# Turning attention heads for a two-layer trunk: per token tile in split form, or two heads at a time as plain float32 rows

## The chip, the cores and the metric

The kernel runs on one core of one Trainium2 chip. The metric is the device time of one execution in microseconds (us), as the median of several runs. TensorE (PE) multiplies matrices, VectorE (DVE), ScalarE (ACT) and GpSimd (POOL) do the elementwise work, and SyncE (SP) issues most of the DMAs. PE writes into PSUM banks of 128 partitions x 512 float32 values; ACT and DVE empty them into SBUF.

## The reference, cut to what matters

Two layers, each a half feed-forward, a mixer and another half feed-forward, on 512 tokens of width 1024 in float32. The mixer projects the normalised input once and feeds three kinds of attention. The change concerns the query and key heads between projection and scores:

```python
proj = h @ w_in
(qa, ka, va, qi, ki, wi, qb, kb, vb, qc, kc, vc, ga, gb, gc) = jnp.split(proj, offsets, axis=-1)
qa = rope(rmsnorm(qa.reshape(B, S, A_HEADS, HEAD_DIM), qk_g[0]), cos, sin)
...
sc = jnp.einsum('bqhcd,bshcd->bhcqs', qb, k) * scale
```

Projection leaves tokens on the partitions and heads along the free dimension. Scores need the head dimension (64) on the partitions and tokens along the free dimension, so every query and key head has to be transposed.

## The kernel before

**Precision.** Matrix products run in the one-pass type float32r. To keep float32 accuracy each operand is carried as two parts, `hi` (the value rounded to float32r) and `lo` (the rest), and a product is the sum of three matmuls (`mm3`, L227 to L229; in the projections L758 to L760).

**Heads.** A turned head is a 128x512 tile `dst[h]`: hi of the 64 head values on one half of the partitions, lo on the other half, tokens along the row. `scores` (L843) multiplies a query tile with the key tile and with a copy whose halves are exchanged by two DMAs (`swapped`, L837), which gives all four products of hi and lo.

**Groups.** Per layer there are five groups of heads: `qi` (8 index queries, token tiles 1 to 3), `ki` (1 index key), `b` (8 heads), `c0` and `c1` (8 each), `a` (5). A group is projected by `project` (L745): for each token tile of 128, 24 matmuls into an `mm` bank, handed out in four pieces of six. Then ACT copies the result out with the norm's scale, the norm of the heads (`normed`, L777) and the rotation (`rope`, L765, on POOL) follow.

**Turning, to_heads (L817).** For each token tile, `lag` turns of the main loop after its projection (4 for `qi` and `ki`, 7 for the others), `split` writes hi with ACT (L822) and lo with DVE (L823) into a tile `st`, [head][hi, lo][64]. Three turns later (`LAG_H`) `turn` transposes each head (L829): one 128x128 float32r transpose per head and token tile, four heads to a PSUM bank `tr`, two banks for eight heads. Each head's 128x128 block is then copied to `dst[h]` by whichever of ACT and DVE is assigned (`nc.any`, L832).

**The main loop** (end of `mixer`) does in each turn: `tick()`, which issues the deferred steps that are due; one unit of attention work if there is credit (index scores, then attention b, c0, c1, a, each when its heads are `ready`); picks of the top-k choice at 0.36 a turn, all on DVE (L1004, L1005); then one piece of dense work, the first in the list `dense` whose condition holds. Everything issued by the first three is held behind the last dense matmul (`behind`), and a planner puts each engine's instructions in a fixed order at build time. Attention transposes its probabilities with plain float32 128x128 transposes (`turned`, L863, transposes at L870, copies at L872), in the same three `tr` banks.

**Buffers.** PSUM has 2 banks `mm`, 3 `sc`, 3 `tr`. `st` has two buffers, the rows `v` of the heads share the tag `t1` (three buffers).

Of the kernel before, what the change touches and what calls it, by code (L numbers as in the profile page):

```python
# [36 lines left out]
T1 = 3  # L37
P0 = 4
P1 = 2
PT = 6  # L40
ST = 2
RAW = 4
QL = 4
HL = 4
# [3 lines left out]
RATE = 1  # L48
PICKS = 0.36
LAG_I, LAG_N = 4, 7  # L50
LAG_S, LAG_H = 4, 3
LAG_T, LAG_C, LAG_V = 3, 5, 2
AHEAD = 4
FF_PARTS = [4, 4, 4, 4, 6]
# [25 lines left out]
def trunk_kernel(ctx, tc, xt_in, pos_in, ng_in, wgu, wdn, wgrp, wgate, wbr_s, wbr_c, wo, qkg_in, lam_in, subg_in, out):  # L80
# [34 lines left out]

    ident = const.tile([P, P], F32, name="ident")
    make_identity(nc, ident)
    ident_r = const.tile([P, P], F32R, name="ident_r")
    V.tensor_copy(ident_r, ident)
# [114 lines left out]
    class Norm:  # L234
# [80 lines left out]
        def diagonals(self):  # L315
            parts = sm.tile([P, 2, NT, 1], F32R, name=nm("rnp"), tag="rnp", bufs=1)
            V.tensor_copy(parts[:, 0], self.rn)
            V.tensor_tensor(parts[:, 1], self.rn, parts[:, 0].bitcast(F32), op=ALU.subtract)
            self.dg = [tmp.tile([P, T], F32R, tag=tag, name=nm("dg"), bufs=b) for tag, b in (("t1", T1), ("t2", 2))]
            for e, dg in enumerate(self.dg):  # L320
                V.tensor_tensor(dg.rearrange("p (t q) -> p t q", t=NT), ident_r[:, None, :].bitcast(F32).to_broadcast([P, NT, P]),
                                parts[:, e].bitcast(F32).to_broadcast([P, NT, P]), op=ALU.mult)

        def broadcast(self):
# [407 lines left out]
    def mixer(l, n, nxt, aside):  # L732
# [44 lines left out]
        def normed(o, t, spec):  # L777

            nh = sum(s[1] for s in spec)
            v = temp("t1", bufs=T1).rearrange("p (h d) -> p h d", d=HD)  # L780
            S.activation(v[:, :nh], o[:, :nh * HD].rearrange("p (h d) -> p h d", d=HD), AF.Copy, scale=n.rn[:, t, :])
            sq = temp("t0")
            S.activation(sq[:, :nh * HD].rearrange("p (h d) -> p h d", d=HD), v[:, :nh], AF.Square)
            ss = sm.tile([P, 8, 1], F32, name=nm("ss"), tag="ss")
            V.reduce_sum(ss[:, :nh, 0], sq[:, :nh * HD].rearrange("p (h d) -> p h d", d=HD), axis=AX.X)
            V.tensor_scalar(ss[:, :nh, 0], ss[:, :nh, 0], 1.0 / HD, EPS, op0=ALU.mult, op1=ALU.add)
            G.tensor_tensor(ss[:, :nh, 0], ss[:, :nh, 0], neghalf[:, :nh], op=ALU.pow)

            def scaled():
                V.tensor_tensor(v[:, :nh], v[:, :nh], ss[:, :nh].to_broadcast([P, nh, HD]), op=ALU.mult)  # L790
                h0 = 0
                for row, hn in spec:
# [21 lines left out]
                for _, fn in due:  # L814
                    fn()

        def to_heads(v, nh, t, dst, lag, done):  # L817

            s = phase[-1].tile([P, 8, 2, HD], F32R, tag="st", name=nm("st"), bufs=ST)

            def split():
                S.activation(s[:, :nh, 0, :], v[:, :nh], AF.Copy)  # L822
                V.tensor_tensor(s[:, :nh, 1, :], v[:, :nh], s[:, :nh, 0, :].bitcast(F32), op=ALU.subtract)  # L823
                defer(LAG_H, turn)

            def turn():
                ps_ = [bank("tr") for _ in range(0, nh, 4)]
                for h in range(nh):
                    PE.transpose(ps_[h // 4][:, h % 4 * P:(h % 4 + 1) * P].bitcast(F32R),  # L829
                                 s[:, h].rearrange("p a d -> p (a d)"), ident_r)  # L830
                for h in sorted(range(nh), key=lambda h: (h % 4, h)):
                    nc.any.tensor_copy(dst[h][:, t * P:(t + 1) * P], ps_[h // 4][:, h % 4 * P:(h % 4 + 1) * P])  # L832
                done[0] += 1

            defer(lag, split)

        def swapped(src):  # L837
            d = slot(F32R)
# [80 lines left out]
        va = phase[-1].tile([P, NT, HD], F32, tag="va", name=nm("va"), bufs=1)  # L919

        def dense_qi():
            for t, o in project("qi", range(1, NT)):
# [4 lines left out]
                v = temp("t1", bufs=T1).rearrange("p (h d) -> p h d", d=HD)  # L927
# [5 lines left out]
        def dense_ki():  # L933
            for t, o in project("ki"):
                if o is None:
                    yield True
                    continue
                v = temp("t1", bufs=T1).rearrange("p (h d) -> p h d", d=HD)
                S.activation(v[:, 0], o[:, :HD], AF.Copy, scale=n.rn[:, t, :])
                rope(v[:, :1], t, 1)  # L940
                to_heads(v, 1, t, kis, LAG_I, ready["i"])
# [4 lines left out]
        ready = {k: [0] for k in ("i", "b", "c0", "c1", "a")}  # L946

        def dense_qk(name, rows, qs, ks):
            for t, o in project(name):
                if o is None:  # L950
                    yield True
                    continue
                v = normed(o, t, [(base + rows[0], 4), (base + rows[1], 4)])
                to_heads(v, 8, t, qs + ks, LAG_N, ready[name])
                yield True

        def dense_vc():
            for t, o in project("vc"):
# [3 lines left out]
                S.activation(vc(t), o, AF.Copy, scale=n.rn[:, t, :])  # L962
                yield True

        def dense_a():
            for t, o in project("a"):
                if o is None:
                    yield True
                    continue
                v = normed(o, t, [(base + 0, 4), (base + 1, 1)])  # L970
                to_heads(v, 5, t, qa + ka, LAG_N, ready["a"])
                S.activation(va[:, t, :], o[:, 320:384], AF.Copy, scale=n.rn[:, t, :])
                yield True

# [172 lines left out]
        def finished(b):  # L1147

            if b not in outs:
# [10 lines left out]
        work = deque([  # L1160
            (lambda: ready["i"][0] == 2 * NT - 1, index_scores()),
            (lambda: ready["b"][0] == NT,
             attend("b", qb, kb, None, causal_mask, lambda j, h: vb(j)[:, h * HD:(h + 1) * HD], on_b)),
            (lambda: ready["c0"][0] == NT, attend_c(qc0, kc0, 0, on_c[:2])),
            (lambda: ready["c1"][0] == NT, attend_c(qc1, kc1, 1, on_c[2:])),
            (lambda: ready["a"][0] == NT and len(masks) == NT,
             attend("a", qa, ka * 4, ka2, lambda i: masks[i], lambda j, h: va[:, j, :], on_a)),
        ])

# [121 lines left out]
```

## Time and profile before

| | |
|---|---|
| median of 3 runs | 2293.15 us (2291.82 to 2294.11) |
| the profiled execution's own time | 2294.2 us |
| its span | 2292.4 us |
| granted TensorE clock over the span | 0.999 of full speed |
| first mixer stage, roughly | 366 to 756 us |
| second mixer stage, roughly | 1502 to 1892 us |

The span is the time from the first to the last recorded instruction. A busy share is the time in which an engine had an instruction under way. Matmuls overlap their neighbours, so a PE that is busy all the time is not by that at its peak; what one block of matmuls costs is read from the starts of the matmuls around it. The two mixer stages run the same program, so one is read and the result doubled.

### The profile page before, as it was taken

To read this page: it belongs to the slowest core of one execution; us is meant where nothing else is said; L and a number is where in the kernel's file an instruction comes from. 1 tells how busy PE (TensorE), PEld (TensorE's weight loads), DVE (VectorE), ACT (ScalarE), POOL (GpSimd) and SP (SyncE) were. 2 spreads that over 40 slices of the span, in tenths; PEclk is the share of its full clock that TensorE was granted. 3 is DMA by queue.
4 is the path that set the end of the run, shared out by engine and by line. 5 is a ranking of instruction groups with operands and counts; after the bars stand their busy time and mean duration, and the time that the engine had idled before them with its cause. 6 is when DMAs were issued, how large, how long until landed. Compare 5 with 4: busy or idle time off the path is not lost.

```text
span 2292.4 us, 35928 instructions
## 1 busy us (share of the span) xinstructions
PE 2266.5 (99%) x13605; PEld 2002.1 (87%) x13605; DVE 1717.4 (75%) x3104; ACT 1110.6 (48%) x2097; POOL 384.7 (17%) x501
## 2 busy tenths in 40 slices
PE   9999999999999999999999999999999999999999
PEld 7899988888888889999889999888888887899997
DVE  7777765798965777777687777658999657777774
ACT  5544435666534454444444444456764344444442
POOL 0111101364011111110011101033631110110100
PEclk9999999999999999999999999999999999999999
DMA  4656525322232455655256555243322224655552
GB/s 169 181 155 162 141 66 168 96 78 84 79 97 82 135 152 154 163 156 141 77 151 166 160 145 158 76 135 83 93 76 91 88 83 138 166 157 149 150 139 65
DMA packets 111646, 286.74 MB, mean 125 GB/s; under 512 B 13168, under 2 KB 13168, under 8 KB 111472
## 3 DMA queue, kind: packets, MB, share of 16 engines
q1 hardware_dynamic: 89584, 245.21, 33.8%
q0 software_dynamic: 20736, 37.76, 9.8%
q8 instruction: 107, 1.75, 0.3%
q10 hardware_dynamic: 1152, 1.47, 0.2%
q14 instruction: 67, 0.55, 0.1%
HBM read 270.76 MB, written 6.29 MB: 121 GB/s over the span
## 4 chain that ended last, share of the span: by engine, by line
PE 86%; DVE 7%; DMA 2%; ACT 2%; issue 1%; POOL 1%; SPq 0%; ACTq 0%; DVEq 0%; POOLq 0%
PE mm L227 11%; PE mm L229 11%; PE mm L228 11%; PE sc L227 8%; PE sc L229 8%; PE sc L228 8%; PE tr L227 5%; PE tr L229 5%; PE tr L228 5%; PE mm L758 3%; PE mm L759 3%; PE mm L760 3%; PE sc L847 1%; PE sc L848 1%; DVE lo L344 1%
## 5 line engine op out<-in xcount | busy, mean ns | idle before, releaser
L227 PE MATMUL mm<-h,hi 128*128 128x512 f32 x1216 | 481.0, 396 | 1.5 <-DVE h L547 0.8
L229 PE MATMUL mm<-h,lo 128*128 128x512 f32 x1216 | 475.3, 391 | 4.3 <-DVE lo L344 4.3
L228 PE MATMUL mm<-h,hi 128*128 128x512 f32 x1216 | 474.4, 390 | 0.0
L452 POOL DMA_DIRECT2D sa<-in_wgu x144 | 126.5, 1050 | 929.9 <-DMA sa<-in_wgu 449.9
L229 PEld LDWEIGHTS mm<-h,lo 128*128 128x128 f32 x1216 | 228.3, 188 | 54.8 <-DVE lo L344 6.1
L344 DVE TENSOR_TENSOR lo<-raw,hi 128x1024 fp32r<-128x1024 f32 (+1 forms) x198 | 232.9, 1179 | 56.1 <-ACT hi L341 55.7
L227 PEld LDWEIGHTS mm<-h,hi 128*128 128x128 f32 x1216 | 228.4, 188 | 47.8 <-issue 3.4
L227 PE MATMUL sc<-h,hi 128*128 128x256 f32 (+1 forms) x832 | 264.9, 318 | 0.0
L228 PEld LDWEIGHTS mm<-h,hi 128*128 128x128 f32 x1216 | 228.6, 188 | 41.2
L229 PE MATMUL sc<-h,lo 128*128 128x256 f32 (+1 forms) x832 | 263.6, 317 | 0.0
L228 PE MATMUL sc<-h,hi 128*128 128x256 f32 (+1 forms) x832 | 263.3, 316 | 0.0
L341 ACT ACTIVATE hi<-raw 128x1024 fp32r<-128x1024 f32 (+1 forms) x198 | 200.5, 1020 | 88.2 <-PE tr L228 56.2
L227 PE MATMUL tr<-h,hi 128*128 128x256 f32 (+1 forms) x704 | 214.3, 304 | 3.7 <-ACT hi L572 1.8
L229 PE MATMUL tr<-h,lo 128*128 128x256 f32 (+1 forms) x704 | 213.6, 303 | 0.0
L228 PE MATMUL tr<-h,hi 128*128 128x256 f32 (+1 forms) x704 | 213.3, 303 | 0.0
L220 ACT ACTIVATE hi<-raw 128x1024 fp32r<-128x1024 f32 (+2 forms) x136 | 139.6, 1029 | 96.1 <-PE mm L228 58.4
L221 DVE TENSOR_TENSOR lo<-raw,hi 128x1024 fp32r<-128x1024 f32 (+2 forms) x136 | 172.7, 1271 | 16.7 <-ACT hi L220 15.9
L227 PEld LDWEIGHTS sc<-h,hi 128*128 128x128 f32 x832 | 158.8, 191 | 12.8 <-ACT hi L572 0.5
L228 PEld LDWEIGHTS sc<-h,hi 128*128 128x128 f32 x832 | 158.9, 191 | 11.9
L229 PEld LDWEIGHTS sc<-h,lo 128*128 128x128 f32 x832 | 158.7, 191 | 10.8 <-DVE lo L573 0.2
L227 PE MATMUL sc<-h,qhi 128*128 128x256 f32 x576 | 162.6, 282 | 4.2 <-ACT e L485 2.2
L758 PE MATMUL mm<-hi,h 128*128 128x512 f32 (+2 forms) x432 | 165.3, 383 | 0.0
(331 smaller groups left out, 5027.8 us busy)
## 6 DMA issues: line engine op xcount, KB each, us to landing
raw<-in_wgu SPq DMA_DIRECT2D x102, 512.0 KB, 4.6
sa<-in_wgu SPq DMA_DIRECT2D x72, 512.0 KB, 3.9
sa<-in_wgu POOLq DMA_DIRECT2D x144, 256.0 KB, 5.9
raw<-in_wdn SPq DMA_DIRECT2D x128, 256.0 KB, 4.0
raw<-in_wgate SPq DMA_DIRECT2D x48, 512.0 KB, 3.6
raw<-in_wgrp SPq DMA_DIRECT2D x40, 512.0 KB, 4.7
a<-in_wgu SPq DMA_DIRECT2D x72, 256.0 KB, 5.0
raw<-in_wdn SPq DMA_DIRECT2D x32, 384.0 KB, 3.7
```

What stands on the lines that cost most here:

```text
L220: S.activation(hi[:, sl], raw[:, sl], AF.Copy)
L221: V.tensor_tensor(lo[:, sl], raw[:, sl], hi[:, sl].bitcast(F32), op=ALU.subtract)
L227: PE.matmul(o, ah, bl, start=first, stop=False, skip_group_check=onto)
L228: PE.matmul(o, ah, bh, start=False, stop=False, skip_group_check=onto)
L229: last_mm[0] = PE.matmul(o, al, bh, start=False, stop=last, skip_group_check=onto)
L341: S.activation(self.h, self.src, AF.Copy)
L344: V.tensor_tensor(self.l, self.src, self.h.bitcast(F32), op=ALU.subtract)
L452: G.dma_start(self.sa[:, j * 512:(j + 1) * 512], src[:, 1536:], accum_op=ALU.add)
L758: PE.matmul(o[:, :w_cols], xl, wh[:, sl], start=k == 0, stop=False)
L759: PE.matmul(o[:, :w_cols], xh, wh[:, sl], start=False, stop=False)
L760: last_dense[0] = PE.matmul(o[:, :w_cols], xh, wl[:, sl], start=False, stop=k == KD - 1)
L847: PE.matmul(o, ql, k2[:, :(i + 1) * P], start=True, stop=False)
```

## The change

The heads are kept as plain float32 rows until all token tiles of a group are there (new tag `hv`, six buffers; for `ki` a slot of the large pool). Then, `lag` turns of the loop after the last tile, one pair of heads is turned in each turn of the loop: for each of the four token tiles (three for `qi`) one float32 transpose of 128 tokens x two heads of 64, all into one `tr` bank, which then holds head h on partitions 0 to 63 and head h+1 on 64 to 127, with all 512 tokens along the row. hi and lo are made while the bank is emptied: ACT copies each half to its place in `dst` (rounded to float32r), DVE subtracts that from the bank and writes lo to the other half of the partitions. Heads at odd places so have hi and lo exchanged, queries and keys alike.

`split`, `st`, `LAG_H` and `ident_r` go. The readiness conditions count heads in place of token tiles. Group `c1` may start only when group `a` has not begun or has all its tiles.

```diff
-        def to_heads(v, nh, t, dst, lag, done):
-            s = phase[-1].tile([P, 8, 2, HD], F32R, tag="st", name=nm("st"), bufs=ST)
-            def split():
-                S.activation(s[:, :nh, 0, :], v[:, :nh], AF.Copy)
-                V.tensor_tensor(s[:, :nh, 1, :], v[:, :nh], s[:, :nh, 0, :].bitcast(F32), op=ALU.subtract)
-                defer(LAG_H, turn)
-            def turn():
-                ps_ = [bank("tr") for _ in range(0, nh, 4)]
-                for h in range(nh):
-                    PE.transpose(ps_[h // 4][:, h % 4 * P:(h % 4 + 1) * P].bitcast(F32R),
-                                 s[:, h].rearrange("p a d -> p (a d)"), ident_r)
-                for h in sorted(range(nh), key=lambda h: (h % 4, h)):
-                    nc.any.tensor_copy(dst[h][:, t * P:(t + 1) * P], ps_[h // 4][:, h % 4 * P:(h % 4 + 1) * P])
-                done[0] += 1
-            defer(lag, split)
+        def head_rows():
+            return phase[-1].tile([P, 8, HD], F32, tag="hv", name=nm("hv"), bufs=HV)
+
+        def to_heads(vs, nh, dst, lag, done):
+            t0, t1 = min(vs) * P, (max(vs) + 1) * P
+            def turn(h):
+                both = h + 1 < nh
+                o = bank("tr")
+                for t, v in vs.items():
+                    PE.transpose(o[:HD * (1 + both), t * P:(t + 1) * P], v[:, h:h + 1 + both].rearrange("p a d -> p (a d)"), ident)
+                rows = slice(0, HD), slice(HD, P)
+                for e in range(1 + both):
+                    S.activation(dst[h + e][rows[e], t0:t1], o[rows[e], t0:t1], AF.Copy)
+                for e in range(1 + both):
+                    V.tensor_tensor(dst[h + e][rows[1 - e], t0:t1], o[rows[e], t0:t1], dst[h + e][rows[e], t0:t1].bitcast(F32),
+                                    op=ALU.subtract)
+                done[0] += 1 + both
+            for h in range(0, nh, 2):
+                defer(lag + h // 2, lambda h=h: turn(h))
...
-                to_heads(v, 8, t, qis, LAG_I, ready["i"])
+                if t == NT - 1:
+                    to_heads(vs, 8, qis, LAG_I, ready["i"])
...
-                 (lambda: units["b"] == 16, dense_qk("c1", (4, 5), qc1, kc1)), (lambda: 1 in outs, gated(1)),
+                 (lambda: units["b"] == 16 and len(rows_a) in (0, NT), dense_qk("c1", (4, 5), qc1, kc1)), (lambda: 1 in outs, gated(1)),
...
-            (lambda: ready["i"][0] == 2 * NT - 1, index_scores()),
-            (lambda: ready["b"][0] == NT,
+            (lambda: ready["i"][0] == 9, index_scores()),
+            (lambda: ready["b"][0] == 8,
```

## Rows read from the trace of the kernel before

**Rows 1.** The page, part 1: busy time, share of the span and instructions by engine.

```profile
PE 2266.5 (99%) x13605; PEld 2002.1 (87%) x13605; DVE 1717.4 (75%) x3104; ACT 1110.6 (48%) x2097; POOL 384.7 (17%) x501
```

**Rows 2.** Busy time by stretch: stretch, its length, each engine's busy us (instructions).

```profile
500.00:566.00 66.00, 63.91 (x368) 53.30 (x366) 59.99 (x168) 44.47 (x132) 37.29 (x53) 1.00 0.33 101
566.00:640.00 74.00, 72.94 (x373) 60.19 (x372) 67.98 (x185) 36.06 (x85) 8.86 (x12) 1.00 0.27 82
```

**Rows 3.** Timeline of PE, an eight-head float32r block: start us, length us, engine, line, tiles.

```profile
375.60 0.79 PE L829 MATMUL tr<-ident_r,st 128*128 128x128 f32 x8
376.23 0.47 PE L758 MATMUL mm<-hi,h 128*128 128x512 f32 x1
376.54 0.39 PE L759 MATMUL mm<-hi,h 128*128 128x512 f32 x1
```

**Rows 4.** Timeline of PE, a block of four plain float32 transposes (probabilities).

```profile
461.54 0.60 PE L870 MATMUL tr<-ident,p 128*128 128x128 f32 x4
461.89 0.48 PE L758 MATMUL mm<-hi,h 128*128 128x512 f32 x1
462.21 0.40 PE L759 MATMUL mm<-hi,h 128*128 128x512 f32 x1
462.44 0.40 PE L760 MATMUL mm<-lo,h 128*128 128x512 f32 x1
```

**Rows 5.** Groups by line and form, 366 to 756 us: count | busy us, mean ns.

```profile
L829 PE MATMUL tr<-ident_r,st 128*128 128x128 f32 x144 | 15.4, 244 | 0.0
L870 PE MATMUL tr<-ident,p 128*128 128x128 f32 x120 | 18.8, 273 | 0.9 <-DVE p L1056 0.9
L872 ACT COPY pt<-tr 128x512 f32<-128x512 f32 x9 | 5.1, 579 | 1.5 <-PE tr L870 1.4
L872 ACT COPY pt<-tr 128x384 f32<-128x384 f32 x8 | 3.7, 472 | 0.9 <-PE tr L870 0.8
L872 DVE COPY pt<-tr 128x384 f32<-128x384 f32 x4 | 2.2, 550 | 0.4 <-PE tr L870 0.4
L872 DVE COPY pt<-tr 128x512 f32<-128x512 f32 x3 | 2.1, 686 | 1.0 <-PE tr L870 0.9
```

**Rows 6.** Busy time by stretch of line L823 alone (the lo part, DVE).

```profile
500.00:566.00 66.00, 4.19 (x7) 1.00 0.33 101
...
sum 390.00, DVE 13.13; mean DVE 2.19
```

**Rows 7.** The same of line L832 (the copies out of the bank): DVE, then ACT.

```profile
500.00:566.00 66.00, 1.11 (x4) 10.41 (x48) 1.00 0.33 101
...
sum 390.00, DVE 8.95 ACT 25.04; mean DVE 1.49 ACT 4.17
```

**Rows 8.** The same of line L822 (the hi part, ACT), 366 to 640 us.

```profile
sum 274.00, ACT 12.52; mean ACT 1.57
```

**Rows 9.** Timeline of PE, where it stood still: [idle us before, what ended it].

```profile
510.76 1.53 PE L897 MATMUL tr<-pt,h 128*64 128x128 f32 x24 [1.21 <-ACT pt L872]
...
547.74 0.30 PE L870 MATMUL tr<-ident,p 128*128 128x128 f32 x1 [0.87 <-DVE p L1056]
...
566.92 0.94 PE L882 MATMUL tr<-h,pt 128*128 128x128 f32 x6 [0.62 <-ACT pt L872]
```

**Rows 10.** The chain that ended last, 500 to 566 us: start us, us, what.

```profile
510.23 0.48 ACT pt L872
...
535.38 0.88 ACT h L832 x6
```

**Rows 11.** Timeline of ACT, the split of the last tile of group a.

```profile
509.76 0.47 ACT L822 ACTIVATE st<-t 128x320 fp32r<-128x320 f32 x1 [1.51 <-POOL t L775]
```

**Rows 12.** Timeline of DVE, three instructions in the stretch of group c1.

```profile
546.65 0.68 DVE L823 TENSOR_TENSOR st<-t,st 128x512 fp32r<-128x512 f32 x1
547.25 0.34 DVE L1056 SCALAR_TENSOR_TENSOR p<-p,f,p 128x128 f32<-128x128 f32 x1
...
550.40 0.76 DVE L1068 TENSOR_SCALAR h<-h,css 128x128 f32<-128x128 f32 x1 [1.02 <-POOL css L1067]
```

**Rows 13.** Timeline of PE, the transposes of the last two tiles of group ki.

```profile
397.86 0.22 PE L829 MATMUL tr<-ident_r,st 128*128 128x128 f32 x1
...
403.45 0.22 PE L829 MATMUL tr<-ident_r,st 128*128 128x128 f32 x1
```

More of the change, by code (lines that the diff above doesn't have):

```diff
@@ L40 @@
 PT = 6
-ST = 2
+HV = 6
 RAW = 4
@@ L50 @@
 LAG_I, LAG_N = 4, 7
-LAG_S, LAG_H = 4, 3
+LAG_S = 4
 LAG_T, LAG_C, LAG_V = 3, 5, 2
@@ L117, in trunk_kernel @@
     make_identity(nc, ident)
-    ident_r = const.tile([P, P], F32R, name="ident_r")
-    V.tensor_copy(ident_r, ident)
     one = const.tile([P, 1], F32, name="one")
@@ L921, in dense_qi @@
         def dense_qi():
+            vs = {}
             for t, o in project("qi", range(1, NT)):
@@ L926, in dense_qi @@
                 n.advance(last_dense[0])
-                v = temp("t1", bufs=T1).rearrange("p (h d) -> p h d", d=HD)
+                v = vs[t] = head_rows()
                 S.activation(v, o.rearrange("p (h d) -> p h d", d=HD), AF.Copy, scale=n.rn[:, t, :])
                 rope(v, t, 8)
-                to_heads(v, 8, t, qis, LAG_I, ready["i"])
+                if t == NT - 1:
+                    to_heads(vs, 8, qis, LAG_I, ready["i"])
                 yield True
         def dense_ki():
+            vs = {}
+            kv = slot()[:, :NT * HD].rearrange("p (t d) -> p t d", d=HD)
             for t, o in project("ki"):
@@ L937, in dense_ki @@
                     continue
-                v = temp("t1", bufs=T1).rearrange("p (h d) -> p h d", d=HD)
+                v = vs[t] = kv[:, t:t + 1]
                 S.activation(v[:, 0], o[:, :HD], AF.Copy, scale=n.rn[:, t, :])
-                rope(v[:, :1], t, 1)
-                to_heads(v, 1, t, kis, LAG_I, ready["i"])
+                rope(v, t, 1)
+                if t == NT - 1:
+                    to_heads(vs, 1, kis, LAG_I, ready["i"])
                 S.activation(vb(t), o[:, 64:320], AF.Copy, scale=n.rn[:, t, :])
@@ L948, in dense_qk @@
         def dense_qk(name, rows, qs, ks):
+            vs = {}
             for t, o in project(name):
@@ L952, in dense_qk @@
                     continue
-                v = normed(o, t, [(base + rows[0], 4), (base + rows[1], 4)])
-                to_heads(v, 8, t, qs + ks, LAG_N, ready[name])
+                vs[t] = normed(o, t, [(base + rows[0], 4), (base + rows[1], 4)])
+                if t == NT - 1:
+                    to_heads(vs, 8, qs + ks, LAG_N, ready[name])
                 yield True
@@ L963, in dense_vc @@
                 yield True
+        rows_a = {}
         def dense_a():
+            vs = rows_a
             for t, o in project("a"):
@@ L969, in dense_a @@
                     continue
-                v = normed(o, t, [(base + 0, 4), (base + 1, 1)])
-                to_heads(v, 5, t, qa + ka, LAG_N, ready["a"])
+                vs[t] = normed(o, t, [(base + 0, 4), (base + 1, 1)])
+                if t == NT - 1:
+                    to_heads(vs, 5, qa + ka, LAG_N, ready["a"])
                 S.activation(va[:, t, :], o[:, 320:384], AF.Copy, scale=n.rn[:, t, :])
@@ L1160, in mixer @@
         work = deque([
-            (lambda: ready["i"][0] == 2 * NT - 1, index_scores()),
-            (lambda: ready["b"][0] == NT,
+            (lambda: ready["i"][0] == 9, index_scores()),
+            (lambda: ready["b"][0] == 8,
              attend("b", qb, kb, None, causal_mask, lambda j, h: vb(j)[:, h * HD:(h + 1) * HD], on_b)),
-            (lambda: ready["c0"][0] == NT, attend_c(qc0, kc0, 0, on_c[:2])),
-            (lambda: ready["c1"][0] == NT, attend_c(qc1, kc1, 1, on_c[2:])),
-            (lambda: ready["a"][0] == NT and len(masks) == NT,
+            (lambda: ready["c0"][0] == 8, attend_c(qc0, kc0, 0, on_c[:2])),
+            (lambda: ready["c1"][0] == 8, attend_c(qc1, kc1, 1, on_c[2:])),
+            (lambda: ready["a"][0] == 5 and len(masks) == NT,
              attend("a", qa, ka * 4, ka2, lambda i: masks[i], lambda j, h: va[:, j, :], on_a)),
```

4 lines of the change are left out of this document (2 added, 2 removed).

## The prediction, made before the result was known

> **What bounds the kernel now.** I read the page's busy times first: PE is busy 99% of the span, DVE 75%, ACT 48% [rows 1]. A busy PE can still be a slow one, so I went to PE's timeline in the first mixer stage and took distances between starts: matmuls of the projections start 0.23 us after one another without holes (462.21 to 462.44, [rows 4]), and the places where PE stood still are few, the largest 1.21, 0.87 and 0.62 us [rows 9]. So PE sets the time nearly everywhere, and work taken from it is worth its own length, as long as the others keep up. That is in doubt in one stretch: from 500 to 640 us DVE is busy 59.99 of 66 us and 67.98 of 74 us [rows 2]; PE's three halts lie there, released by ACT and DVE [rows 9], and the chain that ended last leaves PE and runs over ACT and DVE, over the head copies among others [rows 10]. Both layers have the same two stages, so I work out one mixer and double it.
>
> **PE: the transposes.** A block of eight float32r transposes starts at 375.60, the next matmul at 376.23 and the one behind it at 376.54 [rows 3]. The normal distance is 0.23, so the block costs 0.94 - 0.23 = 0.71 us: 0.63 us, or 0.079 for each transpose, and 0.08 once for the change over. Per layer there are 144 of them [rows 5]: 15 blocks of eight (three tiles of qi, four each of b, c0, c1), four blocks of five (a) and four single ones (ki), 23 blocks. 144 x 0.079 + 23 x 0.08 = 13.2 us.
>
> The new transposes are plain float32, 128 tokens by two heads of 64, which is the form in which the probabilities are turned already, 120 times per layer [rows 5]. Four of these start at 461.54, the matmul after next at 462.21 [rows 4]: 0.67 - 0.23 = 0.44 us for a block of four, change over included. After the change there are four blocks of three (qi; about 0.33 us) and 16 of four (ki 1, b, c0, c1 4 each, a 3): 4 x 0.33 + 16 x 0.44 = 8.4 us. **PE saves 4.8 us per layer, 9.6 us in all.** The two kinds of single-head block (ki, the fifth head of a) have only 64 columns; I price them as full ones, and their error is below 0.2 us a block.
>
> A page speaks against this. The Trainium skill, "FP8 and Floating Point Precision", section TensorE Precision Notes, has true float32 take four passes through the array. Were that so for these transposes, each would cost 4 x 0.079 = 0.32 us, the 76 new ones with 20 change overs 25.6 us per layer, and the kernel would be 25 us slower (an estimate with the page's factor). The row on the same form does not agree: 0.44 us for four.
>
> **ACT: relieved.** It loses the hi part (12.52 us per layer, [rows 8]) and its share of the copies (25.04 us, [rows 7]), 37.6 us. It gets one copy of 64x512 per head (64x384 for qi). The trace has none with 64 partitions; the nearest rows are the copies from the same kind of bank with 128, 0.579 us for 512 columns and 0.472 for 384 [rows 5]; the half of the partitions could cost anything from half of that to the same, and I take the same, because the length of the row is what differs between those two rows. 30 x 0.579 + 8 x 0.472 = 21.1 us: 16 us less per layer. Off the path it is worth nothing by itself; on the chain it stands at a few places only.
>
> **DVE: burdened, and in bursts.** It loses the lo part (13.13 us, [rows 6]) and 8.95 us of copies [rows 7], 22.1 us. It gets 38 subtractions out of PSUM. No row shows one that writes to other partitions than it reads; the nearest rows are 0.686 us for 512 columns out of a bank and 0.550 for 384 [rows 5]. 30 x 0.686 + 8 x 0.550 = 25.0 us, 2.9 us more per layer (between 10 us less, if half the partitions took half the time, and somewhat more). What matters is where: in 500 to 566 us it now has 4.19 + 1.11 = 5.3 us of head work [rows 6, 7]; after, c1 (8) and a (5) put 13 x 0.686 = 8.9 us there, 3.6 us more in a stretch that has 6 us of idle DVE. And the eight of a group no longer come spread over four tiles (16 turns of the loop) but in four turns in a row.
>
> How DVE overlaps its instructions weighs here. The lo part at 546.65 is 0.68 long and the next starts 0.60 later [rows 12], so 0.08 is hidden. The Trainium skill, "VectorE: DVE Perf Modes", section Two Vector instructions with no wait between them, has an instruction start only when all earlier ones have finished if its first partition differs from that of the last one's input or output. The new subtractions jump between the halves, so by it each pair would lose about three overlaps. No run here shows that yet. Three times 0.08 is 0.24 us for a pair, 1.4 us for the six pairs in that stretch; I leave it out of the sum and let it weigh in the rival below.
>
> **Order.** The index scores need the last turn of ki, which came 4 + 3 turns of the loop after its projection and now comes after 4. Two successive transposes of ki lie four turns apart, 397.86 and 403.45 [rows 13], 1.4 us a turn; so the index scores, the picks and all attention start three turns, some 4.2 us, earlier against the dense work. That is no gain to PE, whose total is the same, but it gives DVE a start for the tight stretch. The groups with lag 7 are ready when they were (7 + 3 turns then, the fourth pair at 7 + 3 now). The new condition on c1 costs at most a turn or two: attention b ends by my count within a turn of a's last tile. The six row buffers suffice by the same count: a's third tile needs a row of c0, whose last pair is turned two turns earlier.
>
> **A wait moved.** ACT's split of a's last tile waited 1.51 us for POOL's rotation [rows 11], and the copy behind it in ACT's queue let PE stand 1.21 us [rows 9, 10]. Now the first pair's transposes come at that same lag, and it is PE itself that would wait for POOL, with the projections queued behind it; in turn ACT's queue is free. Between 1.5 us lost and 1.2 us won per layer; I take nothing.
>
> **The sum.** 2294.2 - 9.6 = 2284.6 if all keep up. Against that I set 1.75 us per layer, about half of DVE's 3.6 us, for halts in the tight stretch: its idle time and its earlier start cover part, but much of its idle time is waiting in order on POOL (1.02 us at 550.40, [rows 12]) and can't all be filled. 2294.2 - 9.6 + 3.5 = 2288.1 for the profiled execution, whose time lies 1.05 us above the median; **2287.0 us** against the median, 6 us or 0.27% less.
>
> **The rivals.**
> DVE takes it all back. If the bursts push DVE past PE in c0, a and c1, the added 3.6 us and the 1.4 us of lost overlap land on the path, and the saving after 500 us (c1 and part of a, some 1.5 us) is hidden: 4.8 - 1.5 - 5.0 = -1.7 us per layer at the worst, 2296.5; at the mild end 2288.6. For it speaks the share of DVE, against it its earlier start and ACT's relief. Chance 0.30, no measurable change.
>
> The three tr banks are held too long, and it is slower. A new bank is held for two copies and two subtractions, 2 x 0.579 + 2 x 0.686 = 2.5 us, against some 1.4 us a turn. In four turns (5.6 us, 16.8 us of three banks) a burst needs 4 x 2.5 = 10 and attention's own transposes and products about 3: it fits. It decides at about 1 us of lateness of DVE (4 x 3.5 + 3 = 17); at 2 us late, four banks need 18 + 3 = 21, and PE waits (21 - 16.8) = 4.2 us in place, with all projections behind it. In two of the three bursts that fall into attention (c0, a, c1): 8.4 - 4.8 = 3.6 us per layer, 2300 us; in all three 2308. For it speaks that a burst asks 5.5 us of DVE in four turns on top of a share of 80%; against it, that fewer banks are taken than before (one per pair in place of two per tile). Chance 0.19; the four passes above have 0.01 of it besides, 0.20 for slower.
>
> The relief is worth more than the burden: the halts that ACT caused go (1.21 and 0.62, [rows 9]), and DVE's start covers its burst. 9.6 + 2 x 1.8 = 13.2, 2280 us. Chance 0.10.
>
> **How the numbers follow.** Forecast (2283 to 2288.5) 0.40, relief 0.10, taken back 0.30, slower 0.20. What a measurement of this kernel can tell from no change is about 0.2%, 4.6 us: faster 0.50, same 0.30, slower 0.20. The range leaves out the lower half of the relief case and the upper half of the slower one: 2281 to 2301. The likeliest case alone is 2283 to 2288.5.
>
> **What would show it.** PE: blocks of four at about 0.44 us and 152 of them. DVE: subtractions near 0.69 us and a busy sum some 6 us higher in all; ACT's sum some 33 us lower. First index score some 4 us earlier after ki's last tile. If the halts of PE between 480 and 570 us add up to more than 5 us per layer, with DVE or the tr banks as what ended them, the forecast is wrong. So it is if a transpose of two heads costs clearly more than 0.11 us.

## The result, and the profile after

The changed kernel takes 2336.93 us (2334.16 to 2337.72), before beside it 2294.11 us (2291.82 to 2296.76): a ratio of 1.0185, 95% interval 1.0174 to 1.0197. It is 43 us **slower**; I had forecast 2287.0 and a range up to 2301. The profiled execution has a time of its own of 2334.16 us and a span of 2332.4, at a mean granted clock of 0.994 (before: 2294.2, 2292.4, 0.999).

First the terms that I had priced. The page's part 1 of the changed kernel answers [rows 1]:

```profile
PE 2277.6 (98%) x13469; PEld 2005.4 (86%) x13469; DVE 1725.0 (74%) x3075; ACT 1089.4 (47%) x1897; POOL 384.6 (16%) x501
```

PE has 136 transposes fewer, DVE 7.6 us more, ACT 21.2 us less. PE's time without work over the span grows from 25.9 to 54.8 us. The groups by line and form, whole span (count | busy us, mean ns of one | idle time in front of them), answer [rows 5]:

```profile
L833 DVE TENSOR_TENSOR h<-tr,h 64x512 fp32r<-64x512 f32 x60 | 41.3, 688 | 11.7 <-ACT h L831 10.6
L831 ACT ACTIVATE h<-tr 64x512 fp32r<-64x512 f32 x60 | 35.5, 592 | 22.7 <-PE tr L828 22.2
L828 PE MATMUL tr<-ident,hv 128*128 128x128 f32 x136 | 24.0, 292 | 18.1 <-DVE ss L784 10.5 <-POOL hv L773 7.6
L833 DVE TENSOR_TENSOR h<-tr,h 64x384 fp32r<-64x384 f32 x16 | 8.9, 555 | 6.3 <-ACT h L831 6.1
```

The sizes are as I took them: 688 and 555 ns against 686 and 550 for the subtractions, 592 against 579 for the copies of 512 columns. The new thing stands at the end of the third line: TensorE now waits in front of its transposes, 18.1 us in all. The blocks themselves are short, here group a's in the midst of c1's projections; the last line is of c1's own blocks (timeline of PE, changed kernel):

```profile
588.99 0.60 PE L828 MATMUL tr<-ident,hv 128*128 128x128 f32 x4
589.34 0.48 PE L756 MATMUL mm<-hi,h 128*128 128x512 f32 x1
589.66 0.39 PE L757 MATMUL mm<-hi,h 128*128 128x512 f32 x1
...
610.56 0.90 PE L828 MATMUL tr<-ident,hv 128*128 128x128 f32 x3 [5.24 <-DVE ss L784]
```

From 588.99 to 589.66 are 0.67 us, less the normal distance of 0.23 again 0.44 us for a block of four. So the 43 us are not in the price of a transpose. Most of them, as the experiments below show, come with the order of the work. Line L756 is one of the three projection matmuls; its busy time on PE by stretch shows when projections run (stretch, its length, PE busy us (records), granted clock, DMA share, GB/s). First the kernel before (there the line is L758), then the changed one:

```profile
520.00:540.00 20.00, 8.34 (x20) 1.00 0.08 27
540.00:560.00 20.00, 0.00 (x0) 1.00 0.32 106
...
580.00:600.00 20.00, 0.00 (x0) 1.00 0.44 131
```

```profile
520.00:540.00 20.00, 1.34 (x4) 1.00 0.44 132
540.00:560.00 20.00, 0.00 (x0) 1.00 0.31 85
560.00:580.00 20.00, 0.00 (x0) 1.00 0.22 75
580.00:600.00 20.00, 10.52 (x27) 1.00 0.18 54
600.00:620.00 20.00, 2.22 (x6) 0.91 0.32 105
```

Before, all projections are over by 538 us. Now c1's run from 580.8 to 604 us: the gates of branch 1 (`gated(1)`) have come in front of them, in the midst of group a. What that leaves for later is seen in the windows of the first mixer (PE, PEld, DVE, ACT, POOL busy), the second and third of which answer [rows 2]:

```profile
366.00:500.00 134.00, 128.34 (x689) 109.61 (x689) 93.11 (x213) 71.67 (x139) 57.57 (x88) 0.99 0.29 85
500.00:566.00 66.00, 65.52 (x355) 55.43 (x355) 58.94 (x168) 36.78 (x86) 12.30 (x25) 1.00 0.33 96
566.00:640.00 74.00, 67.98 (x319) 55.37 (x318) 61.65 (x135) 33.09 (x60) 26.89 (x38) 0.98 0.30 89
640.00:700.00 60.00, 52.29 (x301) 42.38 (x302) 45.89 (x152) 32.49 (x94) 12.40 (x12) 0.94 0.14 45
```

The stretch that I feared, 500 to 566 us, is better than before. Most of the loss comes behind it: from 566 to 700 us PE stands still 13.7 us (before: 1.3 us), and its clock falls. Another 5.7 us stand in front of it, from 366 to 500 us, where the kernel before has none. From 640 us on the attention of c1 runs with no dense work left to put between its units, so PE waits for each unit's DVE work. The waits of PE in the changed kernel, whole span (us in total, times, longest), hold four that the kernel before has not, or hardly has (the second one there is L870 on L1056 with 1.7 us), together 31.5 us over both mixers:

```profile
PE tr L828 <- DVE ss L784: 10.5, 2, 5.2
PE tr L873 <- DVE p L1070: 8.2, 8, 1.8
PE tr L828 <- POOL hv L773: 7.6, 4, 2.3
PE tr L873 <- DVE p L1043: 5.2, 8, 1.5
```

The first and the third of them are the same kind of wait. At 610.50 us POOL ends the rotation of c1's third tile (the last part, L773, begins at 610.05 and takes 0.45), and the transposes start at 610.56; the profile names DVE's L784 because that ended 0.04 us later still. So PE stands 18.1 us in front of the new transposes for POOL's rotation.

**The turn that did it.** I followed the loop turn by turn from the code; the turns say when work is issued, and the planner can still move it. Before, the index scores begin in turn 35, attention b ends in turn 94, and a's last tile comes at 92: c1 follows (97 to 109), then `gated(1)` (to 149), and the attention of c1 begins at 123. Changed, ki's transposes come three turns earlier, all attention moves with them, and b ends in turn **91**. a's last tile is due at **92**. So at 91 `rows_a` holds three tiles, the new condition keeps c1 back, the next entry in the list that may run is `gated(1)`, and it stands ahead of a. It runs to turn 130; a's last tile comes at 132, c1 at 136 to 148, the attention of c1 begins at 158 in place of 123. From 149 to 194 the list of dense work has nothing that may run: 46 turns, where before there were 10. The trace has c1 where the count has it; a's last 12 matmuls the planner drew forward, to 520.6 to 522.6 us.

### The profile page after: what moved, and what is told of

It reads as the page before. It is cut to its first block, busy times and chain, and to the rows that moved or that the text cites. A ratio compares the mean times of both kernels' runs of the same rounds, so it can differ in the third digit from the quotient of the medians.

```text
span 2332.4 us, 35503 instructions
## 1 busy us (share of the span) xinstructions
PE 2277.6 (98%) x13469; PEld 2005.4 (86%) x13469; DVE 1725.0 (74%) x3075; ACT 1089.4 (47%) x1897; POOL 384.6 (16%) x501
## 4 chain that ended last, share of the span: by engine, by line
PE 88%; DVE 7%; POOL 2%; DMA 1%; issue 1%; ACT 1%; SPq 0%; DVEq 0%; POOLq 0%; ACTq 0%
PE mm L225 11%; PE mm L227 11%; PE mm L226 11%; PE sc L225 8%; PE sc L227 8%; PE sc L226 8%; PE tr L225 5%; PE tr L226 5%; PE tr L227 5%; PE mm L756 3%; PE mm L757 3%; PE mm L758 3%; PE tr L873 1%; DVE lo L219 1%; DVE p L860 1%
## 5 line engine op out<-in xcount | busy, mean ns | idle before, releaser
L342 DVE TENSOR_TENSOR lo<-raw,hi 128x1024 fp32r<-128x1024 f32 (+1 forms) x198 | 233.0, 1179 | 55.4 <-ACT hi L339 54.8
L756 PE MATMUL mm<-hi,h 128*128 128x512 f32 (+2 forms) x432 | 164.7, 381 | 0.0
```

The costliest lines, as they stand in the source:

```text
L342: V.tensor_tensor(self.l, self.src, self.h.bitcast(F32), op=ALU.subtract)
L756: PE.matmul(o[:, :w_cols], xl, wh[:, sl], start=k == 0, stop=False)
```

## The experiments

Times are medians beside the kernel before on the same chip; the ratios are to that.

### Is it the order?

Three kernels. The first holds `gated(1)` back by the same condition as c1 (e1). The second gives ki its old place, three turns later, which restores the old order entirely (e2). The third is the kernel before with `gated(1)` in front of c1 in the list, old transposes (e3).

```diff
e1:  -  (lambda: 1 in outs, gated(1)),
     +  (lambda: 1 in outs and len(rows_a) in (0, NT), gated(1)),
e2:  -  to_heads(vs, 1, kis, LAG_I, ready["i"])
     +  to_heads(vs, 1, kis, LAG_I + 3, ready["i"])
e3:  -  (lambda: units["b"] == 16, dense_qk("c1", (4, 5), qc1, kc1)), (lambda: 1 in outs, gated(1)),
     +  (lambda: 1 in outs, gated(1)), (lambda: units["b"] == 16, dense_qk("c1", (4, 5), qc1, kc1)),
```

> The changed kernel, with one condition added: gated(1) too starts only when group a has not begun or has all its tiles. By a count of the main loop's turns, attention b is done at turn 91 and a's last tile comes at turn 92, so that in the changed kernel gated(1), whose condition holds and which stands ahead of a in the list, runs its 40 turns first and c1 waits for a behind it. Theory 1 (order of the dense work): c1 starts right after a again, near 510 us, the halts of 5.2 us and those between 630 and 665 us go, and the time is 2283 to 2295 us. Rival 2 (PE waits for POOL's rotation in front of each group's transposes, and DVE's bursts): these do not depend on c1's place, so most of the 43 us stay, 2320 to 2337 us.

> The changed kernel, with ki turned three turns later (lag 7 in place of 4), so that the index scores and all attention begin in the same turn of the loop as before the change; by the count attention b is then done at turn 94, two turns after a's last tile, and the order of the dense work is that of the kernel before. Theory 1 (order): about as e1, 2283 to 2297 us. Rival 2 (POOL and DVE halts): 2320 to 2337 us. Beside e1 it tells whether an earlier start of the index scores is worth anything: e1 ahead by up to 8 us if it is.

> The kernel before, heads turned as they were, with gated(1) moved ahead of c1 in the list of dense work, as it came out in the changed kernel: c1 by the count at turns 134 to 149 in place of 94 to 109. Theory 1 (order): this alone costs most of it, 2320 to 2345 us, with the clock granted below 1 near the end of the mixer. Rival 2: the old way of turning has no burst and no wait of PE on POOL, so it stays within 8 us of the kernel before, 2290 to 2302 us.

Measured: e1 2307.52 us, ratio 1.0062 (1.0045 to 1.0078). e2 2296.29 us, 1.0017 (1.0007 to 1.0026). e3 2319.66 us, 1.0116 (1.0101 to 1.0131). The order alone makes the old transposes 27 us slower (e3), and taking it out of the changed kernel gives some 28 us back (e1, by the ratios). But e1 lies between the ranges of its two theories: the order is most of the 43 us and not all. e2 shows what is left with the order of before: still 4 us slower, where I had counted 9.6 us of gain. Between e1 and e2 lie 11 us, for the three turns by which the index scores are issued earlier. I had called that "a start for the tight stretch". On the chip it is hardly a start. In e1 ki's transposes come 2.0 us earlier than in e2 (399.19 against 401.23 us), but then PE stands for the DMAs that exchange the halves of ki, and the first scores begin within 0.2 us of each other (timeline of PE, e1, then e2):

```profile
405.62 0.36 PE L850 MATMUL sc<-h,h 128*128 128x256 f32 x1 [1.01 <-DMA h<-h]
```

```profile
405.80 0.28 PE L850 MATMUL sc<-h,h 128*128 128x256 f32 x1
```

From 366 to 760 us PE stands still 11.4 us in e1 and 7.2 in e2, which for two mixers is 8.4 of the 11 us; of the 4.2 us in one mixer 2.9 lie before 500 us.

### Is it one turn?

By the count of turns, ki one turn later (b ends at 92) still lets `gated(1)` in first, and two turns later (93) doesn't.

```diff
e11: -  to_heads(vs, 1, kis, LAG_I, ready["i"])
     +  to_heads(vs, 1, kis, LAG_I + 1, ready["i"])
e12: +  to_heads(vs, 1, kis, LAG_I + 2, ready["i"])
```

> The changed kernel with ki's transposes one turn of the loop later (lag 5 in place of 4). By the count of turns attention b then ends at turn 92, while a's last tile becomes due in that same turn and its first matmuls are drawn behind gated(1): the order stays as in the changed kernel (gated(1) first, a's last tile at 132, attention c1 at 158). If the slowdown hangs on that order: 2330 to 2340, as the changed kernel. If it is the early start of the index scores in itself, it falls by a third of what three turns bring: 2320 to 2325.

> The changed kernel with ki's transposes two turns later (lag 6). By the count attention b ends at turn 93, one turn behind a's last tile (92): c1 goes ahead of gated(1) as before, attention c1 at 122. One turn more than in the run before should then bring some 35 us at once: 2296 to 2306. If the slowdown grows evenly with the earliness of the index scores: 2308 to 2312, half way.

Measured: 2343.48 us (1.0217, 1.0202 to 1.0233) and 2302.71 us (1.0038, 1.0023 to 1.0053). **One turn of the loop is 41 us.** The same windows of L756, one turn later, then two:

```profile
560.00:580.00 20.00, 1.52 (x4) 1.00 0.22 57
580.00:600.00 20.00, 10.41 (x26) 1.00 0.22 76
600.00:620.00 20.00, 1.17 (x3) 0.74 0.34 105
```

```profile
520.00:540.00 20.00, 8.26 (x20) 1.00 0.02 2
540.00:560.00 20.00, 0.00 (x0) 0.91 0.42 130
...
580.00:600.00 20.00, 0.00 (x0) 1.00 0.33 91
```

In the first c1's projections lie between 578 and 602 us, in the second in front of 540. The step is where the count puts it. The rival, that the whole time falls evenly with the turn of the index scores, is out. Among the kernels with the right order it does fall: 2307.5 us with turn 32 (e1), 2302.7 with 34 (e12), 2296.3 with 35 (e2). Part of the step is PE's clock, 0.989 in e11's profiled execution against 0.997 in e12's, some 26 against 7 us by the sum given in the last section. That one turn later is some 7 us slower even than the changed kernel, which no theory had, goes with longer halts in the same place. When c1 is projected there, the attention of c0 has ended (turn 121), and by the count the turns 149 to 154 hold neither dense work nor attention, so the lag of seven turns behind c1's last tile covers little; the gates that the planner has kept back stand behind these transposes in PE's order. PE comes to them while POOL still rotates c1's third tile, until 611.62 us (timeline of PE, one turn later):

```profile
611.67 1.33 PE L828 MATMUL tr<-ident,hv 128*128 128x128 f32 x5 [7.89 <-POOL hv L773]
```

In the changed kernel the same halt is 5.24 us long: there c1's projections end 1.9 us later (604.0 against 602.1 us) and that rotation 1.1 us earlier.

### Is the early start bad by itself?

The kernel before, with ki split one turn earlier and transposed one turn behind the split in place of three, so that the index scores begin in turn 32.

```diff
e7:  -  to_heads(v, 1, t, kis, LAG_I, ready["i"])
     +  to_heads(v, 1, t, kis, LAG_I - 1, ready["i"], 1)      # the last: turns from split to transposes, in place of LAG_H
```

> The kernel before, heads turned as they were, but ki split three turns after its projection and transposed one turn later, four turns in all, so that the index scores and all attention start three turns earlier, as in the changed kernel. There is no guard on c1, so by the count c1 and gated(1) both go ahead of a's last tile, which comes after them. Theory 1 (the place of the attention work against the dense work is what costs, not the way of turning): 2297 to 2307 us. Rival 2 (the earlier start is harmless where c1 keeps its place): 2290 to 2296 us.

Measured: 2308.05 us, 1.0065 (1.005 to 1.008), as e1, and 1 us above the first theory's range. But it isn't the early start alone: without the condition, c1's first 12 matmuls now stand ahead of a's last 12 on PE (not all of c1 and `gated(1)`, as I had expected by the count). Its halts are of another kind: the projections, and a gate behind them, wait for their bank, behind ACT's row copy.

```profile
536.15 0.50 PE L758 MATMUL mm<-hi,h 128*128 128x512 f32 x1 [1.40 <-ACT t L781]
546.20 0.80 PE L227 MATMUL mm<-h,hi 128*128 128x512 f32 x1 [2.04 <-ACT t L781]
```

So I take from it only that a start three turns earlier is no help with the old transposes either. Why it costs there, I can't say further than that PE's halts get longer.

### Where do the 9.6 us go, with the order right?

The halts of PE in e2's first mixer, then what stands in DVE's queue ahead of the copy that the second one waits for (timelines):

```profile
430.94 0.33 PE L828 MATMUL tr<-ident,hv 128*128 128x128 f32 x1 [1.78 <-POOL hv L773]
...
534.59 1.24 PE L885 MATMUL tr<-h,pt 128*128 128x128 f32 x6 [2.14 <-DVE pt L875]
```

```profile
529.97 0.69 DVE L788 TENSOR_TENSOR hv<-hv,ss 128x512 f32<-128x512 f32 x1 [0.98 <-POOL ss L785]
...
532.08 0.75 DVE L1082 TENSOR_SCALAR h<-h,css 128x128 f32<-128x128 f32 x1 [0.75 <-POOL css L1081]
...
534.00 0.54 DVE L875 COPY pt<-tr 128x384 f32<-128x384 f32 x1
```

The first is PE waiting in its own queue for the rotation of the group's last tile. The second is DVE, late because it waited twice, in order, for POOL. By stretch (PE busy, e2):

```profile
366.00:500.00 134.00, 131.70 (x720) 1.00 0.30 89
500.00:566.00 66.00, 62.15 (x333) 0.97 0.29 88
```

PE stands still 2.3 us before 500 us (before: 0) and 3.9 us from 500 to 566 us (before: 2.1). Behind the second halt the granted clock is 0.54, 0.50, 0.50 and 0.76 in the four us from 535 to 539, which takes 1.7 us more.

First I moved the two halts: a lag of nine turns for the normed groups (e4), all copies of the probabilities on ACT (e5), both (e6).

```diff
e4:  -  LAG_I, LAG_N = 4, 7
     +  LAG_I, LAG_N = 4, 9
e5:  -  nc.any.tensor_copy(pt[:, :w], p[:, :w])
     +  S.activation(pt[:, :w], p[:, :w], AF.Copy)
```

> e2 (the changed kernel with ki turned three turns later, so that the dense work has its old order), and LAG_N 9 in place of 7: the first pair of a normed group is transposed nine turns after its last tile, so that PE finds the rows rotated. All heads are still ready before attention asks for them by the count of turns. Theory 1: what e2 lost against its saving of 9.6 us is PE standing in front of the transposes for POOL's rotation (1.78 and 0.96 us in the first mixer), each halt with a lower clock behind it; these go, 2288 to 2293 us. Rival 2: the loss is DVE's bursts; with the pairs only moved, not thinned out, it stays, 2294 to 2299 us.

> e2, and the copy of the turned probabilities out of their bank always on ACT, in place of the planner's choice. In e2 the largest halt of PE in the first mixer, 2.14 us, waited for such a copy on DVE, which stood in DVE's queue behind an instruction that waited for POOL; the clock fell behind it. Theory 1 (DVE's queue is what PE waits for now, while ACT has 16 us per layer less to do): 2288 to 2293 us. Rival 2 (ACT is as late as DVE, since both wait in order): 2294 to 2299 us.

> e2 with both: LAG_N 9 and the probabilities copied on ACT. If the halts of e2 are these two and nothing takes their place, most of the 9.6 us is left: 2283 to 2289 us, faster than the kernel before. If DVE simply paces this stretch (rival), the halts move to other instructions: 2292 to 2299 us.

Measured: 2306.08 us (1.0054, 1.0038 to 1.0071), 2295.57 us (1.0019, 1.0001 to 1.0037), 2299.1 us (1.0025, 1.0016 to 1.0035). None helps; e4 is some 9 us slower than e2, beyond both of its theories. With the longer lag the waits for POOL are gone and others stand in their place (e4's timeline of PE):

```profile
504.84 0.41 PE L873 MATMUL tr<-ident,p 128*128 128x128 f32 x2 [2.38 <-DVE p L1043]
...
537.52 0.94 PE L885 MATMUL tr<-h,pt 128*128 128x128 f32 x6 [1.33 <-DVE pt L875]
```

A wait that is moved says nothing on its price. So next I took work away, each on top of e2: two kinds of DVE work given to ACT (e8, and the same on the kernel before, e9), subtractions of 64 columns (e10), no rotation of the last tile (e13), and all three (e14). The kernels e10, e13 and e14 leave part of the computation out and serve as probes only.

```diff
e8:   -  V.tensor_scalar(pr[:, :(i + 1) * P], pr[:, :(i + 1) * P], rd, None, op0=ALU.mult)
      +  S.activation(pr[:, :(i + 1) * P], pr[:, :(i + 1) * P], AF.Copy, scale=rd)
      -  V.tensor_scalar(to, o, r0, None, op0=ALU.mult)
      +  S.activation(to, o, AF.Copy, scale=r0)
e10:  -  V.tensor_tensor(dst[h + e][rows[1 - e], t0:t1], o[rows[e], t0:t1], ...)
      +  V.tensor_tensor(dst[h + e][rows[1 - e], t0:t0 + 64], o[rows[e], t0:t0 + 64], ...)
      +  nc.sync.dma_start(dst[h + e][rows[1 - e], t0 + 64:t1].bitcast(F32), dst[h + e][rows[e], t0 + 64:t1].bitcast(F32))
e13:  -  rope(v[:, :nh], t, nh)
      +  if t < NT - 1:
      +      rope(v[:, :nh], t, nh)
```

> The new turning with the dense order of before (as in e2), and two kinds of VectorE work given to ScalarE: the normalizing of the probabilities (L1043, 32 a layer at 0.28 to 0.99 us, median 0.41) and the first scaling behind attention c (L1076, 16 a layer at 0.34). That takes some 18 us a layer from VectorE, about 12 of them between 450 and 640 us, where it is busy 129 of 140. If VectorE's queue is what eats the 9.6 us that TensorE saves, the time falls below before's: 2284 to 2290. If it is the chain through GpSimd, the clock, or the long chains in themselves, the halts stay: 2294 to 2300. If ScalarE is by then as tight, 2300 or more.

> The kernel before with the same two kinds of VectorE work given to ScalarE. Before's TensorE is short of 134+66+74 us by only 3 in the three stretches from 366 to 640, so if VectorE is no bound there, this changes nothing: 2290 to 2295, and the difference from e8 is what the new turning is worth with VectorE relieved (9.6 less by the count of TensorE's work). If this falls as much as e8 does against e2, VectorE's queue held both kernels alike, and is no reason for the difference between e2 and before.

> The new turning with the dense order of before (as in e2), but each subtraction across the halves (L833) takes 64 columns only, and a DMA copies the remaining columns of the first half in their place: the scores are no longer split exactly, which is left out of the computation. VectorE loses 38 x some 0.4 = 15 us a layer, all of it in the blocks that the change made. If those blocks on VectorE eat the gain, 2283 to 2289; if it is the order of the chains (the wait for GpSimd and for the last tile), as e2: 2294 to 2299; the added DMAs (38 a layer on SP's queue) can cost some us by holding up the loads of the weights.

> As e2 (the changed kernel with the dense order of before), but the rotation on GpSimd is left out for the last token tile of groups b, c0, c1 and a; their scores are not the reference's. It takes away what the first pair's transposes wait for, with no lag moved. If TensorE's wait for GpSimd (1.8 + 1.0 us a layer, and some 0.5) is a loss of its own: 2296 - 6 = 2289 to 2291. If it only hides that VectorE is late, the halts come back on VectorE's lines as with the longer lag: 2294 to 2298.

> As e2, with everything at once that could hold TensorE back: no rotation of the last tile (e13), subtractions of 64 columns with a DMA for the rest (e10), normalizing on ScalarE (e8). The split and the last tile's rotation are left out of the computation. If TensorE's saving of 4.8 us a layer is real and is eaten by these waits alone, it shows here: 2282 to 2287. If the new transposes themselves cost TensorE more than I counted: 2290 or more, with few halts left in its timeline.

| | us | ratio to before | against e2 |
|---|---|---|---|
| e2 | 2296.29 | 1.0017 (1.0007 to 1.0026) | |
| e8, less on DVE | 2294.53 | 1.0006 (0.9997 to 1.0016) | -0.0011 |
| e10, short subtractions | 2293.02 | 1.0000 (0.9991 to 1.0009) | -0.0017 |
| e13, no last rotation | 2293.58 | 1.0000 (0.9990 to 1.0010) | -0.0017 |
| e14, all three | 2288.50 | 0.9980 (0.9971 to 0.9989) | -0.0037 |
| e9, before with e8's edit | 2297.74 | 1.0024 (1.0014 to 1.0034) | |

Each single one disappoints: e8 stays where I expected it if VectorE isn't the cause, e10 and e13 end between the numbers of their two theories. Each ratio is good to about 0.001, so e8's gain isn't clear of the noise and those of e10 and e13 only just. Together they are clear: 0.0037, some 8.5 us, where the single ones sum to 0.0045. So VectorE's subtractions and POOL's rotation seem to hold a part of the loss each; how much belongs to which, these runs don't show. The transposes' waits are gone from e14 (groups by line: e2, then e14, where the line is L829):

```profile
L828 PE MATMUL tr<-ident,hv 128*128 128x128 f32 x136 | 22.2, 276 | 6.9 <-POOL hv L773 5.5 <-DVE h L833 1.4
```

```profile
L829 PE MATMUL tr<-ident,hv 128*128 128x128 f32 x136 | 21.3, 274 | 1.1 <-DVE h L834 1.1
```

So much of TensorE's saving is there, but against the kernel before only 4.5 us of it come out even so. e14's first mixer still has halts at the attention's copies:

```profile
540.29 1.16 PE L887 MATMUL tr<-h,pt 128*128 128x128 f32 x8 [1.39 <-DVE pt L877]
```

From 366 to 760 us I summed what each distance between PE's starts has over its normal pitch (0.23 us for 512 columns, 0.11 for a float32 transpose, 0.079 for an old one): 12.3 us in e14 against 11.2 in the kernel before, some 1 us a layer (0.3 to 1.8, by how the short excesses are counted). That leaves some 3 us of the 9.6 which I haven't located.

The baseline is in doubt as well. e8's edit made the kernel before 5 us slower (e9, where I had expected no change), so it isn't a pure relief. With that edit on both sides the new turning is 3 us ahead of the old one (e8 against e9); e14 would be 10 us ahead of e9, as much as the count of transposes says, but it does less work than e9. The share of the 9.6 us that is lost for good stays open.

### Can the waits be taken away with the whole computation kept?

On top of e8: normalization and rotation begun a turn earlier (e15, `LAG_S` 3), or transposes a turn later (e16, `LAG_N` 8).

```diff
e15:  -  LAG_S = 4
      +  LAG_S = 3
e16:  -  LAG_I, LAG_N = 4, 7
      +  LAG_I, LAG_N = 4, 8
```

> e8 (new turning, dense order of before, normalizing on ScalarE) with the normalization and rotation of each tile begun one turn of the loop earlier (LAG_S 3 in place of 4), the transposes at the same lag. If that gives GpSimd the turn (some 1.6 us) that TensorE waited for (1.78 + 0.46 + 1.14 us in e8's first mixer): 2288 to 2291. If VectorE's scaling then waits longer for the power on GpSimd, and its queue behind it: 2294 to 2298.

> e8 with the transposes of b, c0, c1 and a one turn later (lag 8 in place of 7). The count of turns keeps the order of all attention and dense work, and a's third tile (88) still finds c0's rows turned (87). TensorE's waits for GpSimd in e8's first mixer (1.78 + 0.46 + 1.14) should go: 2288 to 2291. If the halts only move, as with lag nine, 2295 to 2302.

Measured: e15 2321.42 us (1.0119, 1.0104 to 1.0134), e16 2295.45 us (1.0007, 0.9998 to 1.0017). Neither beats the kernel before. e15 is far beyond both of its theories, e16 ends in the range of "the halts only move". The first shows how dear a wait in order is: DVE reaches its scaling before POOL has the power and stands there, POOL's queue then runs the rotation first, and the small `css` behind it comes late for DVE again. First two rows of DVE, then one of PE:

```profile
546.76 0.69 DVE L788 TENSOR_TENSOR hv<-hv,ss 128x512 f32<-128x512 f32 x1 [1.54 <-POOL ss L785]
...
552.04 0.28 DVE L1082 TENSOR_SCALAR h<-h,css 128x128 f32<-128x128 f32 x1 [2.71 <-POOL css L1081]
```

```profile
554.91 2.07 PE L885 MATMUL tr<-h,pt 128*128 128x128 f32 x8 [4.79 <-DVE pt L875]
```

## Why the prediction was wrong, step by step

**Order: the step that failed.** "The new condition on c1 costs at most a turn or two: attention b ends by my count within a turn of a's last tile." The count was right within that turn, and the turn was what mattered: b ends one turn *before* the last tile, and then it isn't c1 that waits a turn or two, it is `gated(1)` that goes ahead for 40 turns. I asked what the condition delays, and not what the list offers in its place. Worth some 28 us (the changed kernel against e1), and 41 us between two neighbouring turns (e11, e12). In the same step I called the earlier index scores a help for DVE. In the changed kernel the first score came 2.9 us earlier (404.55 us against 407.43) and not 4.2, and PE waited 1.49 us for a DMA in front of it. Putting ki's transposes back gives 11 us (e1 against e2).

**A wait moved: mis-sized.** "Between 1.5 us lost and 1.2 us won per layer; I take nothing." PE does wait for POOL's rotation now: 5.5 us over both mixers in e2, 18.1 in the changed kernel. Without the last tile's rotation e2 gets some 4 us faster by the ratios (e13).

**Halts: right in the tight stretch, missing elsewhere.** I set 1.75 us per layer for 500 to 640 us. There PE stands still 4.7 us in e2 against 3.2 before, 1.5 us more, near what I set. What I had at nothing are the 2.3 us in front of 500 us, 1.8 of them for POOL, and the 1.7 us of lower clock. PE's excess over the pitch, summed as above, is 17.3 us in e2 against 11.2, some 6 us a layer (5 to 6): no less than the 4.8 us of gain. The rival "DVE takes it all back" ended at 2296.5 us at its worst, and e2 is at 2296.29: with the order of before, that rival's time would have come true. Its mechanism is at most half right: short subtractions give some 4 us by the ratios (e10, just clear of the noise), so the bursts seem to be part of it, beside POOL's waits and the clock.

**The transposes: right in the block, high in the sum.** A block of four takes 0.44 us (588.99 to 589.66), as [rows 4] had it. The rival of four passes, 0.32 us each, didn't come. Of 9.6 us, 4.5 were seen against the kernel before with the waits eased.

**ACT and DVE prices: right.** Half the partitions cost as much as all: the rows' length sets it, 592 and 688 ns for 512 columns on 64 partitions, against 579 and 686 on 128 [rows 5]. ACT's lines fell by 31.8 us over both layers (75.1 us of the old copies and splits gone [rows 7, 8], 43.3 new), where I had 33; the page's total, which counts overlapped instructions once, fell by 21.2. That ACT's relief was worth nothing, as I had it, no run tests.

**The banks: not seen.** The rival of the slower side had three `tr` banks held too long. The wait of a transpose for a bank is 1.8 us in e2 in all (L828 for L833 1.4, the attention's L873 for L833 0.4); the slowdown had another cause than the one that I priced.

## What to carry to other kernels

Where a list hands out the first piece of work that may run, a new condition on one entry is a permission for the next one: write down the turn in which each condition turns true, before and after, and treat a margin of one turn as none. A change that moves one producer by three turns moves everything that hangs on it; keep the old dates first, then measure the parts. And to price a wait, take away the work that it waits for; moving the wait only shows that another stands next to it.

## What the runs showed of the hardware

**Some halts cost twice.** Behind some halts PE's clock falls to its lower level for some 3 us. The halt, on the timeline of the changed kernel, and windows of 1 us around it, PE busy (records), granted clock:

```profile
654.08 0.55 PE L873 MATMUL tr<-ident,p 128*128 128x128 f32 x3 [1.84 <-DVE p L1070]
```

```profile
652.00:653.00 1.00, 0.23 (x3) 1.00 0.00 0
653.00:654.00 1.00, 0.00 (x0) 1.00 0.09 20
654.00:655.00 1.00, 0.92 (x7) 0.89 0.65 233
655.00:656.00 1.00, 0.91 (x4) 0.50 0.66 270
656.00:657.00 1.00, 1.00 (x7) 0.50 0.49 53
...
658.00:659.00 1.00, 0.91 (x6) 0.91 0.44 176
```

PE stood still 1.84 us until 654.08, after it had been busy 0.44 and 0.48 us in the two us from 650 to 652, and then worked at 0.50 (1.2 GHz) from about 655 to 658. Behind e2's halt of 1.78 us at 430.94 no fall shows (mean 1.00 from 366 to 500 us). The Trainium skill, "TensorE: Matmul & The Clock Gate", section Part 1, has the gate that follows the array's activity pass the clock at half or full rate and at nothing between; the windows agree, with 0.50 or 1.00 but for the edges. By the mean clocks, (1 - 0.994) x 2332.4 = 14 us are lost so in the changed kernel and (1 - 0.999) x 2292.4 = 2 us before (each to about 1 us, as the clock has three digits): some 12 of the 43 us in the profiled execution. I had no term for it.

**Subtractions across the halves don't overlap.** Six of 64x384 in a row in e2 (timeline of DVE):

```profile
383.15 3.40 DVE L833 TENSOR_TENSOR h<-tr,h 64x384 fp32r<-64x384 f32 x6 [0.18 <-ACT h L831]
```

At 555 ns each they start (3.40 - 0.555) / 5 = 0.569 us apart, where the old ones hid 0.08 us [rows 12]. The Trainium skill, "VectorE: DVE Perf Modes", section Two Vector instructions with no wait between them, has an instruction held that starts in another quadrant than the one before it; this row agrees.
